# Decode scores: feature blocks and cache blocks on separate partition groups, 256 keys a product

## The chip, the cores and the metric

The kernel runs on one core of a Trainium2 chip, as one program. The metric is the device time of that core in microseconds, as the median over several runs. Beside it stands one execution that was taken with the hardware profiler; all durations of single instructions come from that one. The engines are TensorE (PE in the profile, with its weight loads as PEld), VectorE (DVE), ScalarE (ACT), GpSimd (POOL) and SyncE (SP).

## The reference

One layer of a hybrid decoder computes a prompt of 512 tokens and 8 sample requests of 4 tokens each: a first SwiGLU, a mixer that has a gated linear recurrence and a latent attention side by side, and a second SwiGLU. What the change touches is the latent attention of the sample tokens over their cache:

```python
s = (jnp.einsum('bqhr,bsr->bhqs', ql, c_kv) + jnp.einsum('bqhd,bsd->bhqs', qr, k_rope)).astype(jnp.float32) * scale
s = jnp.where(k_pos[None, None, None, :] <= qp[None, None, :, None], s, -jnp.inf)
p = jax.nn.softmax(s, axis=-1).astype(c_kv.dtype)
return jnp.einsum('bhqs,bsr->bqhr', p, c_kv)
```

For each of the 8 requests there are 16 queries (4 tokens times 4 heads) against 4096 cached keys. A key has 256 latent features and 64 rotary ones, and the latent part is also the value. The cache lies in pages, so its rows are gathered.

## The kernel before, in words

The decode attention is cut into 16 halves: half `n` has 2048 keys of request `n // 2`, as two gathered cache blocks of 1024 keys. In a block each of the 128 partitions holds 8 cache rows. The class `Half` has its steps, and a generator (`decode`) calls them in a fixed round: while half n is being scored, half n+1 is being transposed and half n-1 gets its softmax and its values.

- `turn` (L1480, tile `kh`): VectorE transposes the gathered rows in squares of 32, so that features come to lie on partitions. The 320 features are ten feature blocks of 32, taken two at a time in five stages; the rotary pair is stage 0. There are two transposes a stage (one per cache block), ten a half, and four `kh` buffers.
- `score` (L1492, tile `s`): TensorE multiplies 64 partitions of queries (two groups of 32 features, arranged as a block diagonal) by the transposed keys. One product has a weight of 64 x 32 and 128 moving columns (four cache rows of 32 keys). The array is used as eight separate tiles, two by partitions of the operands (`r`) and four by output partitions (`c`). All ten feature blocks accumulate into the same output partitions, and the four output groups are the four quarters of a half's keys. That makes 10 x 4 x 2 = 80 products a half, in two runs: stages 0 to 2 (48 products) and stages 3 and 4 (32). The profile records each of these products as two passes with a weight load each, so a run of 48 stands there as 96.
- The end of `score` (L1498, L1500): ScalarE copies the result of one `r` and VectorE that of the other out of PSUM into one tile `e` of 128 x 256 (the profile names it `q`, after the buffer in which it lies); VectorE takes the maximum (`mxh`).
- `peak` (L1504 to L1516): a product spreads the maxima (`pm`), VectorE reduces them and forms the bias (L1506, L1509), ScalarE takes the exponential (L1510), VectorE transposes it (`pt`, L1512), and 16 small copies place it into `pbuf`, twelve on ScalarE and four on VectorE.
- `value` (L1525, tile `o`): 16 products with `pbuf` as the weight and 256 latent columns of the gathered rows.

In between, the same engines work off the second SwiGLU of the prompt, whose generator is advanced beside the decode: products `acc` at L247, weight splits by ScalarE and VectorE (L220, L221), and the gating (`sit`, `sil`, L740 to L754). Later the prompt's remaining feed-forward columns follow as a block scheme with seven products (tiles X, Y, Z), in both kernels alike.

Each engine executes its own list in order. The order in these lists is set when the program is recorded: a layer below the code places an instruction by modelled durations, so an edit also moves its neighbours. `tc.issue_after` ties a transpose to the maximum before it. Nothing outside the decode differs in order between the two kernels, apart from line numbers.

Of the kernel before, what the change touches and what calls it, by code (L numbers as in the profile page):

```python
# [8 lines left out]
F32 = mybir.dt.float32  # L9
# [5 lines left out]
ALU = mybir.AluOpType  # L15
AX = mybir.AxisListType

P = 128
# [42 lines left out]
JS = ((8, 9), (0, 1), (2, 3), (4, 5), (6, 7))  # L61
# [45 lines left out]
def hybrid_step_kernel(  # L107
# [5 lines left out]
    nc = tc.nc  # L113
# [12 lines left out]
    def mk(shape, dt, tag, bufs=1, pool=None):  # L126
        return (pool or cur[-1]).tile(shape, dt, name=tag, tag=tag, bufs=bufs)
# [10 lines left out]
    def ps(name, tag="ps", own=False):  # L138
        if tag == "ps" and not own:
            tag = CYC[turns[0] % 4]  # L140
            turns[0] += 1
        return pp.tile([P, 512], F32, name=name, tag=tag, bufs=NPS[tag])
# [402 lines left out]
    with scope("ffn0") as pool:  # L545
# [4 lines left out]
        l, r = [u[:, lo4] for u in ux], [u[:, hi4] for u in ux]  # L550
# [56 lines left out]
        if True:  # L607
            if True:
                sst.close()
                st = stg.enter_context(tc.tile_pool(name="st", bufs=1, side="right", reuse_waits="tile"))  # L610
# [195 lines left out]
    with scope("mix") as mx_:  # L806
# [291 lines left out]
        with scope("at2"):  # L1098
# [166 lines left out]
            def qsplit(b):  # L1265
                q = qbd[b % 2]
                bs = slice(b * 16, b * 16 + 16)
                for g in range(4):
                    gs = slice(g * 32, g * 32 + 32)
                    (nc.scalar.copy if g % 2 else nc.vector.tensor_copy)(q[gs, :, g % 2 * 16 : g % 2 * 16 + 16], qrep[gs, :, bs])  # L1270
# [131 lines left out]
    with scope("dec"):  # L1402
# [48 lines left out]
        class Half:  # L1451
# [31 lines left out]
            def score(self, st):  # L1483
                q = qbd[self.b % 2]
                if st == 0:
                    self.s = [ps("s", own=True) for _ in range(2)]
                for jj, j in enumerate(JS[st]):
                    for c in range(4):
                        for r in range(2):
                            rs = slice(r * 64, r * 64 + 64)  # L1490
                            kh = self.kh[st][rs, c // 2, c % 2 * 4 : c % 2 * 4 + 4, jj]
                            nc.tensor.matmul(self.s[r][c * 32 : c * 32 + 32, :P], q[rs, j], kh, start=st + jj == 0, stop=st == len(JS) - 1 and jj == 1, skip_group_check=True)  # L1492
                if st == 1 and self.i and self.b + 1 < NB:
                    qsplit(self.b + 1)
                if st < len(JS) - 1:
                    return
                for r in range(2):
                    (nc.vector.tensor_copy if r else nc.scalar.copy)(self.e[:, r * P : r * P + P], self.s[r][:, :P])  # L1498
                self.mx = mk([P, 1], F32, "mxh", 2)
                self.top = nc.vector.tensor_reduce(self.mx, self.e, axis=AX.X, op=ALU.max)  # L1500

            def peak(self):
                pm = ps("pm", "pm")[:, :P]
                nc.tensor.matmul(pm, self.mx.broadcast_to([P, P]), ident, start=True, stop=True, skip_group_check=True)  # L1504
                m = m3[:, self.i, self.bs]
                nc.vector.tensor_reduce(m, pm.rearrange("p (g q) -> p q g", q=16), axis=AX.X, op=ALU.max)  # L1506
                mq = mk([P, 16], F32, "mq", 2)
                mb = mk([P, 1], F32, "mbd", 2)
                nc.vector.scalar_tensor_tensor(mq, m, -SCALE, selL, op0=ALU.mult, op1=ALU.mult, accum_out=mb)  # L1509
                nc.scalar.activation(self.e, self.e, AF.Exp, scale=SCALE, bias=mb, accum_out=Lc[:, self.i, 0, self.b : self.b + 1])  # L1510
                pt = mk([P, ROWS, 32], F32, "pt", 2)
                nc.vector.transpose(pt.rearrange("p a k -> p (a k)"), self.e)  # L1512
                for c in range(4):
                    for g in range(4):
                        src = pt[c * 32 : c * 32 + 32, g // 2 * 4 : g // 2 * 4 + 4, g % 2 * 16 : g % 2 * 16 + 16]
                        (nc.scalar.copy if g else nc.vector.tensor_copy)(self.p[g * 32 : g * 32 + 32, c // 2, c % 2 * 4 : c % 2 * 4 + 4, self.i * 16 : self.i * 16 + 16], src)  # L1516

            def value(self, mate, c):
                i = self.i
# [199 lines left out]
    with scope("ffn1") as pool:  # L1719
# [93 lines left out]
        st = stg.enter_context(tc.tile_pool(name="st2", bufs=1, side="right", reuse_waits="tile"))  # L1813
# [113 lines left out]
```

## Time and profile before

| What | Value |
|---|---|
| Median of 3 runs | 1243.49 us (1242.12 to 1243.71) |
| The profiled execution's own time | 1234.27 us |
| Its span in the trace | 1231.3 us |
| TensorE busy by the records | 98% of the span |
| VectorE, ScalarE, GpSimd busy | 80%, 57%, 8% |
| First and last score product | 724.9 us and 920.5 us of the span |

A row of grouped instructions reads: line, engine, operation, output and inputs, sizes, count, then the busy time in us and the mean of one in ns, and after the second bar the idle time of the engine before these instructions and what ended it. In the chain of waits and in the timeline the first two numbers are the start and the duration in us. In rows of windows each engine has its busy time and its count of instructions; the last three numbers are the granted clock of TensorE, the busy share of the DMA engines and GB/s.

### The profile page before, as it was taken

Reading aid. Unit: us, or ns where it says so; the run is one execution under the profiler, and the core shown is the slowest. Engines: PE = TensorE matmul, PEld = TensorE weight load, DVE = VectorE, ACT = ScalarE, POOL = GpSimd, SP = SyncE. Lnnn points to the kernel's source line nnn. Section 1 sums busy time; section 2 is a strip of 40 time slices with the busy share of each in tenths; the row PEclk is TensorE's granted clock in tenths of the full one; section 3 lists DMA queues with packets and bytes.
Section 4 is the critical chain, followed back from the end, with each engine's and each line's share of the span. In section 5 each row is a group of like instructions: output and inputs, shape, how many; then the busy total and the mean of one; then the engine's idle time right before and its main releaser. Section 6 shows DMA issues by size and latency. Waiting matters only on the chain.

```text
span 1231.3 us, 29416 instructions
## 1 busy us (share of the span) xinstructions
PE 1201.7 (98%) x12204; PEld 1109.0 (90%) x12204; DVE 987.3 (80%) x2008; ACT 705.6 (57%) x1527; POOL 94.2 (8%) x106
## 2 busy tenths in 40 slices
PE   8999999999999999999999999999999999999997
PEld 7999999999999989998998886767777999999996
DVE  7997787878678788886877789888985879768765
ACT  6765545454466754555758765656554455554373
POOL 0000000000000000000000123333320101000000
PEclk9999999999999999999999899999999999999999
DMA  6233333223254313333242686679765666833451
GB/s 240 69 121 103 104 104 97 93 88 101 78 200 136 105 59 103 88 97 114 83 139 88 212 304 224 231 264 357 266 243 184 248 256 236 212 105 115 107 148 73
DMA packets 80518, 190.69 MB, mean 155 GB/s; under 512 B 14064, under 2 KB 37648, under 8 KB 75904
## 3 DMA queue, kind: packets, MB, share of 16 engines
q1 hardware_dynamic: 58128, 115.50, 28.6%
q0 software_dynamic: 16368, 65.67, 16.4%
q10 hardware_dynamic: 5888, 7.65, 1.8%
q8 instruction: 95, 1.56, 0.5%
q14 instruction: 39, 0.32, 0.1%
HBM read 172.63 MB, written 16.16 MB: 153 GB/s over the span
## 4 chain that ended last, share of the span: by engine, by line
PE 79%; issue 7%; DVE 6%; DMA 4%; ACT 3%; POOL 0%; SPq 0%; DVEq 0%; ACTq 0%; POOLq 0%
PE acc L247 18%; PE dn L229 11%; PE Y L448 10%; PE acc L229 8%; PE X L448 7%; PE Z L448 7%; PE acc L1829 3%; PE acc L625 3%; PE s L1492 3%; PE o L1525 2%; DVE kh L1480 2%; DMA ma<-w_g 1%; PE pa L970 1%; DMA mb<-w_d 1%; DMA wraw<-w_g 1%
## 5 line engine op out<-in xcount | busy, mean ns | idle before, releaser
L247 PE MATMUL acc<-uh,wh 128*128 128x272 f32 (+2 forms) x496 | 160.7, 324 | 0.5 <-ACT uh L194 0.5
L247 PE MATMUL acc<-ul,wh 128*128 128x272 f32 (+2 forms) x496 | 156.4, 315 | 0.9 <-DVE ul L195 0.9
L247 PE MATMUL acc<-uh,wl 128*128 128x272 f32 (+2 forms) x496 | 155.5, 314 | 0.8 <-DVE wl L221 0.8
L229 PE MATMUL dn<-hh,dh 128*128 128x272 f32 x384 | 111.3, 290 | 0.1
L229 PE MATMUL dn<-hh,dl 128*128 128x272 f32 x384 | 110.7, 288 | 0.0
L229 PE MATMUL dn<-hl,dh 128*128 128x272 f32 x384 | 110.5, 288 | 0.0
L221 DVE TENSOR_TENSOR wl<-wraw,wh 128x1024 fp32r<-128x1024 f32 (+2 forms) x78 | 83.8, 1076 | 31.8 <-ACT wh L220 31.4
L220 ACT CAST wh<-wraw 128x1024 fp32r<-128x1024 f32 (+2 forms) x78 | 72.6, 932 | 59.8 <-PE acc L247 52.2
L247 PEld LDWEIGHTS acc<-uh,wh 128*128 128x128 f32 x496 | 93.4, 188 | 14.5 <-issue 10.2
L247 PEld LDWEIGHTS acc<-ul,wh 128*128 128x128 f32 x496 | 93.4, 188 | 7.0 <-issue 1.6
L247 PEld LDWEIGHTS acc<-uh,wl 128*128 128x128 f32 x496 | 93.3, 188 | 6.3 <-DVE wl L221 1.0
L229 PEld LDWEIGHTS dn<-hh,dh 128*128 128x128 f32 x384 | 72.3, 188 | 1.1 <-DVE ha L497 0.3
L229 PEld LDWEIGHTS dn<-hl,dh 128*128 128x128 f32 x384 | 72.4, 188 | 0.0
L229 PEld LDWEIGHTS dn<-hh,dl 128*128 128x128 f32 x384 | 72.2, 188 | 0.0
L157 ACT CAST wh<-wraw 128x512 fp32r<-128x512 f32 (+1 forms) x68 | 41.2, 644 | 44.2 <-PE Z L448 29.1
L157 ACT CAST sh<-wraw 128x512 fp32r<-128x512 f32 (+1 forms) x67 | 41.0, 650 | 31.2 <-PE Z L448 19.1
L157 ACT CAST dh<-wraw 128x512 fp32r<-128x512 f32 x48 | 29.7, 620 | 47.0 <-PE dn L229 43.7
L158 DVE TENSOR_TENSOR wl<-wraw,wh 128x512 fp32r<-128x512 f32 (+1 forms) x68 | 46.7, 718 | 6.3 <-ACT wh L157 5.1
L1516 ACT COPY pbuf<-pt 32x64 f32<-32x64 f32 x192 | 46.5, 242 | 7.9 <-DVE pt L1512 5.0
L1492 PE MATMUL s<-kh,q 64*32 64x128 f32 x2560 | 48.3, 273 | 2.5 <-issue 2.5
L1492 PEld LDWEIGHTS s<-kh,q 64*32 64x32 f32 x2560 | 37.3, 105 | 14.8 <-issue 9.2
L158 DVE TENSOR_TENSOR sl<-wraw,sh 128x512 fp32r<-128x512 f32 (+1 forms) x67 | 47.0, 726 | 1.4 <-ACT sh L157 0.8
(721 smaller groups left out, 4114.7 us busy)
## 6 DMA issues: line engine op xcount, KB each, us to landing
wraw<-w_u SPq DMA_DIRECT2D x44, 512.0 KB, 3.9
wraw<-w_g SPq DMA_DIRECT2D x43, 512.0 KB, 3.9
wraw<-w_d SPq DMA_DIRECT2D x24, 512.0 KB, 4.2
wraw<-w_in SPq DMA_DIRECT2D x24, 512.0 KB, 3.4
wraw<-w_o SPq DMA_DIRECT2D x16, 512.0 KB, 3.5
wraw<-w_d SPq DMA_DIRECT2D x16, 384.0 KB, 3.5
wraw<-w_d SPq DMA_DIRECT2D x16, 256.0 KB, 4.3
mA<-sit ACTq DMA_DIRECT2D x14, 256.0 KB, 4.7
```

Source lines behind the costliest of these rows:

```text
L157: nc.scalar.copy(hi, src)
L158: (eng or nc.vector).tensor_tensor(lo, src, f32(hi), op=ALU.subtract)
L220: nc.scalar.copy(wh[:, :kt], w[:, :kt])
L221: low[0] = nc.vector.tensor_tensor(wl[:, :kt], w[:, :kt], f32(wh[:, :kt]), op=ALU.subtract)
L229: nc.tensor.matmul(out, a, b, start=n == 0, stop=n == last)
L247: nc.tensor.matmul(acc[:, :n], a[:, k], b[:, k], start=k + i == 0, stop=k == kt - 1 and i == 2)
L448: nc.tensor.matmul(bank, a[p][:, k], b[q][:, k], start=first and k + n == 0, stop=k == 3 and n == 2, skip_group_check=True)
L625: nc.tensor.matmul(accs[x, d], wts[d][p][:, k], hs[k // 2][q][:, k % 2, x], start=k + n == 0, stop=k == nf - 1 and n == 2)
L1480: nc.vector.transpose(kh[:, g].rearrange("p a j k -> p a (j k)"), src)
L1492: nc.tensor.matmul(self.s[r][c * 32 : c * 32 + 32, :P], q[rs, j], kh, start=st + jj == 0, stop=st == len(JS) - 1 and jj == 1, skip_group_c ...
L1516: (nc.scalar.copy if g else nc.vector.tensor_copy)(self.p[g * 32 : g * 32 + 32, c // 2, c % 2 * 4 : c % 2 * 4 + 4, self.i * 16 : self.i * ...
L1829: nc.tensor.matmul(accs[x, d], wts[d][p][:, k], hs[k // 2][q][:, k % 2, x], start=k + n == 0, stop=k == nf - 1 and n == 2)
```

## The change

The score products are cut in another way. Even and odd feature blocks of a stage (`jj`) go to different output partitions, 0 to 63 and 64 to 127, and within these the two cache blocks (`g`) have 32 partitions each. A product then takes all eight rows of a cache block, 256 columns, and a half has 10 x 2 x 2 = 40 products instead of 80, still on eight tiles of the array. The two partial sums are added at the end: ScalarE copies the odd one out of PSUM into a new tile `odd` (64 x 256, once per `r`), and VectorE adds it to the even one while it writes `e`. The layout of `e` changes with it, and the placing takes 8 copies of twice the size (six on ScalarE, two on VectorE) instead of 16.

```diff
                 for jj, j in enumerate(JS[st]):
-                    for c in range(4):
+                    for g in range(2):
+                        c = (2 * jj + g) * 32
                         for r in range(2):
                             rs = slice(r * 64, r * 64 + 64)
-                            kh = self.kh[st][rs, c // 2, c % 2 * 4 : c % 2 * 4 + 4, jj]
-                            nc.tensor.matmul(self.s[r][c * 32 : c * 32 + 32, :P], q[rs, j], kh, start=st + jj == 0, stop=st == len(JS) - 1 and jj == 1, skip_group_check=True)
+                            nc.tensor.matmul(self.s[r][c : c + 32, : 2 * P], q[rs, j], self.kh[st][rs, g, :, jj], start=st == 0, stop=st == len(JS) - 1, skip_group_check=True)
...
+                odd = mk([64, 2, 2 * P], F32, "odd")
                 for r in range(2):
-                    (nc.vector.tensor_copy if r else nc.scalar.copy)(self.e[:, r * P : r * P + P], self.s[r][:, :P])
+                    nc.scalar.copy(odd[:, r], self.s[r][64:, : 2 * P])
+                    nc.vector.tensor_tensor(self.e[r * 64 : r * 64 + 64], self.s[r][:64, : 2 * P], odd[:, r], op=ALU.add)
...
-                for c in range(4):
-                    for g in range(4):
-                        src = pt[c * 32 : c * 32 + 32, g // 2 * 4 : g // 2 * 4 + 4, g % 2 * 16 : g % 2 * 16 + 16]
-                        (nc.scalar.copy if g else nc.vector.tensor_copy)(self.p[g * 32 : g * 32 + 32, c // 2, c % 2 * 4 : c % 2 * 4 + 4, self.i * 16 : self.i * 16 + 16], src)
+                for r in range(2):
+                    for g in range(2):
+                        for h_ in range(2):
+                            src = pt[(2 * r + g) * 32 : (2 * r + g) * 32 + 32, :, h_ * 16 : h_ * 16 + 16]
+                            to = self.p[(2 * r + h_) * 32 : (2 * r + h_) * 32 + 32, g, :, self.i * 16 : self.i * 16 + 16]
+                            (nc.scalar.copy if g + h_ else nc.vector.tensor_copy)(to, src)
```

On TensorE, at the second run of the first half (about 732 us of the span), the 32 score products stand in pieces between products of the feed-forward network. Before:

```order
L1492 MATMUL s<-kh,q_8213 32x128 x5
L247 MATMUL acc<-ul,wh 128x256
L247 MATMUL acc<-uh,wl 128x256
L247 MATMUL acc<-uh,wh 128x256
L1492 MATMUL s<-kh,q_8213 32x128 x2
```

Now:

```order
L1492 MATMUL s<-kh,q_8213 32x256
L247 MATMUL acc<-uh,wh 128x256
L1492 MATMUL s<-kh,q_8213 32x256 x4
L247 MATMUL acc<-ul,wh 128x256
L247 MATMUL acc<-uh,wl 128x256
L247 MATMUL acc<-uh,wh 128x256
L1492 MATMUL s<-kh,q_8213 32x256 x2
```

The run was five pieces (5, 2, 1, 1 and 23 products); it is now six (1, 4, 2, 1, 1 and 7). In the third half the second run also is in two pieces now, 2 and 14, where it was one of 32; in the second half a run that was in two pieces (42 and 6) is one of 24.

On VectorE, at the seventh half (about 807 to 810 us), from the transposed exponential to the next maximum, before:

```order
L1512 STREAM_TRANSPOSE pt<-q_8213 128x256
L1516 COPY pbuf<-pt 32x4x16 x4
L1480 STREAM_TRANSPOSE kh<-hb 128x512
L1480 STREAM_TRANSPOSE kh<-mb 128x512
L1480 STREAM_TRANSPOSE kh<-rraw 128x512 x2
L1498 COPY q_8213<-s 128x128
L1500 TENSOR_REDUCE mxh<-q_8213 128x1
```

Now:

```order
L1514 STREAM_TRANSPOSE pt<-q_8213 128x256
L1480 STREAM_TRANSPOSE kh<-hb 128x512
L1520 COPY pbuf<-pt 32x8x16 x2
L1480 STREAM_TRANSPOSE kh<-mb 128x512
L1480 STREAM_TRANSPOSE kh<-rraw 128x512 x2
L1500 TENSOR_TENSOR q_8213<-s,odd 64x256 x2
L1502 TENSOR_REDUCE mxh<-q_8213 128x1
```

Two copies stand between the transposes instead of four copies ahead of them, and two additions stand where one copy stood.

On ScalarE, at the same place, before:

```order
L1510 ACTIVATE q_8213<-q_8213,mbd 128x256
L1516 COPY pbuf<-pt 32x4x16 x12
L1498 COPY q_8213<-s 128x128
L1528 COPY q_8248<-o 128x256
L220 CAST wh<-wraw 128x512
```

Now:

```order
L1512 ACTIVATE q_8213<-q_8213,mbd 128x256
L1520 COPY pbuf<-pt 32x8x16 x6
L1499 COPY odd<-s 64x256 x2
L1532 COPY q_8248<-o 128x256
L220 CAST wh<-wraw 128x512
```

Six copies instead of twelve precede two copies of the new tile instead of one copy of the old one.

## The prediction

> **What bounds the kernel now.** I read the head of the page first, then the windows of the decode, then the chain of waits through them, then the groups of instructions and the DMA queues.
>
> ```profile
> span 1231.3 us, 29416 instructions
> PE 1201.7 (98%) x12204; PEld 1109.0 (90%) x12204; DVE 987.3 (80%) x2008; ACT 705.6 (57%) x1527; POOL 94.2 (8%) x106
> ...
> q8 instruction: 95, 1.56, 0.5%
> ```
>
> TensorE is busy 98% of the span, so an edit pays only as far as it shortens TensorE's list or the gaps in it. The windows show where the decode leaves gaps:
>
> ```profile
> 725.00:770.00 45.00, 41.27 (x696) 30.42 (x693) 42.97 (x103) 25.24 (x70) 12.11 (x11) 1.00 0.67 227
> 770.00:897.00 127.00, 123.82 (x2382) 91.30 (x2376) 110.86 (x252) 71.48 (x214) 40.63 (x41) 1.00 0.80 280
> 897.00:935.00 38.00, 37.34 (x591) 25.95 (x576) 29.20 (x72) 20.73 (x60) 6.32 (x8) 1.00 0.60 207
> 1070.00:1197.00 127.00, 127.00 (x1011) 126.43 (x1010) 96.53 (x175) 69.22 (x131) 5.12 (x4) 1.00 0.46 126
> ```
>
> The clock is full throughout. From 725 to 770 VectorE is busy 42.97 of 45 us and TensorE lacks 3.73 us: VectorE bounds there. From 770 to 897 TensorE lacks 3.18 us of 127 and VectorE is busy 87%. From 897 to 935 TensorE lacks 0.66 us. The last row, a stretch behind the decode, has no gap.
>
> In the chain of waits, the middle stretch is one TensorE piece after another:
>
> ```profile
> 782.12 1.52 PE s L1492 x96
> 783.64 2.98 PE acc L247 x12
> 786.62 1.08 PE s L1492 x64
> 787.70 1.86 PE o L1525 x32
> ...
> 821.90 2.01 issue
> ...
> 837.40 0.42 issue
> ...
> 872.68 0.50 issue
> ...
> 885.45 0.24 issue
> ```
>
> A half is a score run of 96 passes (1.52 us), products of the feed-forward network, a run of 64 (1.08), the values (1.86), more products. The four rows "issue" add up to 3.17 us, which is the whole gap of that stretch. No engine or tensor is waited for. What else began just ahead of them? In the view of the DMA queues, over 770 to 897 and then over four windows of 0.1 us each, from 821.5, 835.5, 870.7 and 883.2:
>
> ```profile
> q8 instruction: 19, 0.31, 1.0%
> ...
> q8 instruction: 1, 0.02, 59.8%
> q8 instruction: 1, 0.02, 55.4%
> q8 instruction: 1, 0.02, 65.0%
> q8 instruction: 1, 0.02, 59.4%
> ```
>
> Queue q8 carries TensorE's program. The page has 95 of its packets for 24408 TensorE records, one for 257; the stretch has 19 for 4758, one for 250. Each gap ends 2.3 to 2.4 us after the one packet in its window started (823.91 after 821.5, 837.82 after 835.5, 873.18 after 870.7, 885.69 after 883.2). So these are **waits for code**: the next block had not arrived. Dense score passes are what makes it late. Here a block lasts 127 / 19 = 6.7 us on average; in the stretch from 1070, at 1011 passes with their loads in 127 us, one lasts some 16 us, and nothing is lost.
>
> **The change, part by part.**
>
> *Score products, streaming.* Half as many, each with twice the columns. What does one cost?
>
> ```profile
> 805.10 1.59 PE L1492 MATMUL s<-kh,q 64*32 64x128 f32 x96
> ...
> 810.80 1.07 PE L1525 MATMUL o<-q,pbuf 128*32 128x256 f32 x16
> 811.68 1.05 PE L1525 MATMUL o<-ha,pbuf 128*32 128x256 f32 x16
> ```
>
> The 96 passes are 12 rounds of eight array tiles; less a tail of about 0.2 us, 1.32 / 12 = 0.11 us a round of 128 columns. The value products have 256 columns on four array tiles: 16 of them are four rounds, and the second group starts 0.88 us after the first, 0.22 us a round. So a round costs by its columns. Twelve rounds of 0.11 become six of 0.22, and I expect no gain in streaming. What changes is the ends: the last passes of a run of 96 come at the rate at which they are fed (1.32 / 96 = 14 ns each), which matters less with half as many, but the last round drains 0.11 us longer. For the run of 64, 1.08 us, I get 4 x 0.22 + 0.15 = 1.03; for the run of 96, 6 x 0.22 + 0.15 = 1.47. I take 0.06 us a run, 30 runs: **-1.8 us**, with bounds of -3.6 (0.12 each, if the feeding falls away wholly) and +3.0 (0.1 each, if only the longer drain is felt).
>
> By the Trainium skill (TensorEngine Tiling (Array Packing), Instruction Overhead) every matmul has an overhead of about 60 cycles; at 2.4 GHz that would make 1280 fewer passes worth 32 us, an estimate from that page, against 1.8 by the rows. This trace does not bear it out for passes on eight array tiles: 96 take 1.52 us, 16 ns each with everything in it.
>
> *Code.* 1280 passes and 1280 loads go, 2560 of TensorE's records, ten blocks. In the middle stretch a half now has about 450 records (19 x 250 over 10.5 halves) and will have about 290. Its densest 256 then take some 9 us, where the whole average was 6.7. In the four misses the packet started 0.2 to 2 us too late for a block that lasted about 6 us; with 9 us none of them is a miss. The four gaps are 3.17 us as recorded; a score pass is recorded with 273 ns though another could start 14 ns later, so each hides up to 0.25 us more: **-3.9 us**. Bounds: 0 (the misses only move to other blocks) and -3.9.
>
> The Trainium skill (Runtime: NRT & Kernel Launch, Instruction fetch mechanics) also has code arrive in blocks of 256 instructions, and says that the fetch is hidden by the rate of issue. By the rows above the blocks agree and the hiding does not; if it held, the four gaps would be something else and this term nothing (a rival below).
>
> *End of a score, placing.* The rows, from the groups between 724 and 921 us:
>
> ```profile
> L1516 ACT COPY pbuf<-pt 32x64 f32<-32x64 f32 x180 | 43.6, 242 | 7.7 <-DVE pt L1512 5.0
> L1516 DVE COPY pbuf<-pt 32x64 f32<-32x64 f32 x60 | 11.1, 184 | 1.0
> L1500 DVE TENSOR_REDUCE mxh<-q 128x1 f32<-128x256 f32 x15 | 6.3, 419 | 3.3 <-ACT q L1498 2.6
> L1498 DVE COPY q<-s 128x128 f32<-128x128 f32 x15 | 4.1, 275 | 3.4 <-PE s L1492 3.3
> L1498 ACT COPY q<-s 128x128 f32<-128x128 f32 x15 | 3.9, 262 | 10.0 <-PE s L1492 9.1 <-ACT sit L762 0.8
> L1270 ACT COPY q<-q 32x160 f32<-32x160 f32 x12 | 3.9, 322 | 0.3
> L1270 DVE COPY q<-q 32x160 f32<-32x160 f32 x12 | 2.9, 241 | 3.1 <-PE s L1492 3.0
> L1528 ACT COPY q<-o 128x256 f32<-128x256 f32 x7 | 2.6, 373 | 7.7 <-PE o L1525 7.7
> L788 DVE TENSOR_TENSOR sil<-sil,acc 128x256 f32<-128x256 f32 x1 | 0.4, 416 | 0.0
> ```
>
> ScalarE per half: two copies of 256 columns from PSUM (373 each) and six placing copies (at most 322, the 160-column form) for one of 262 and twelve of 242: 746 + 1932 - 262 - 2904 = -0.49 us. VectorE: two additions (416) and two copies (241) for one of 275 and four of 184: 832 + 482 - 275 - 736 = +0.30 us. And VectorE's list stands still longer at the first addition: from the last product to the maximum it was a copy and the reduction, 0.28 + 0.42; it becomes two ScalarE copies in sequence, the second addition and the reduction, 0.37 + 0.37 + 0.42 + 0.42, **0.9 us later**. Queued behind on VectorE are the next half's six transposes, for which TensorE's next score waits, and weight splits for L247.
>
> Who feels it? In the middle stretch:
>
> ```profile
> PEld s L1492 <- DVE kh L1480: 1.8, 5, 0.4
> ...
> 809.15 1.26 DVE L1480 STREAM_TRANSPOSE kh<-rraw 128x512 f32<-128x512 f32 x2
> 809.60 1.00 PEld L1492 LDWEIGHTS s<-kh,q 64*32 64x32 f32 x64 [0.37 <-DVE kh L1480]
> ```
>
> Some second runs start right as their last transposes end, so there VectorE has no slack. Against the 0.9 + 0.3 us stand the shorter placing ahead of these transposes (0.74 to 0.48) and the list in which the maximum of `pm` now goes ahead of gating work. Spread over 10.5 halves VectorE rises from 87% to about 90% of a stretch that also is 4 us shorter. I take **+1.0 us**, bounds 0 and +6 (seven halves at the full 0.9).
>
> *First halves.* TensorE's pieces:
>
> ```profile
> 731.71 0.36 PE s L1492 x10
> ...
> 732.62 0.34 PE s L1492 x4
> ...
> 733.51 0.33 PE s L1492 x2
> ```
>
> A piece of one product costs 0.33 us, nearly all of it the way in and out; with 256 columns it costs two rounds of 0.22 + 0.11, 0.55 us. The first half's second run has five such short pieces and one of seven, +1.2 us; the third half's extra piece +0.6, and the second half's joined run -0.3. That delays VectorE, which bounds there and has 0.3 us more to do in each of three halves; part is filled by a weight split that now stands ahead of the additions. I take **+1.5 us** (0 to +3).
>
> *Last half.* Its values wait for placing copies, in the waits from 925 to 935:
>
> ```profile
> PEld o L1525 <- ACT pbuf L1516: 2.5, 4, 0.7
> ```
>
> TensorE's own gap there is the 0.66 us of the third window; six copies instead of twelve take it: **-0.6 us** (0 to -0.7).
>
> Later rows move along whole: the order outside the decode is unchanged.
>
> *Sum:* -1.8 - 3.9 + 1.0 + 1.5 - 0.6 = **-3.8 us**. The profiled execution took 1234.27 us, 2.97 more than its span; it would take 1230.5. The median of the runs shown is 9.2 us above that execution; I carry the difference over unchanged, 1243.49 - 3.8 = **1239.7 us**, and count the 9 us as a reason for a wider range.
>
> **The rivals.**
>
> *VectorE takes the pace* (slower). The 0.9 us later maximum costs in every half where transposes end as the score starts. For: 87% busy, 42.97 of 45 us in the first stretch, and the row at 809.60. Against: `PEld s` waits for `kh` are 1.8 us in the whole decode, and the additions come right after a run, with 5 us until the next. It decides once the slack of the next score is under 0.9 us in more than about five halves. Price at ten halves: 0.9 x 10 = +9, the code gap then is half hidden (-2), -1.8, +1.5 - 0.6: 1243.49 + 6 = about 1249; at six halves about 1246.
>
> *The code gaps stay* (nothing visible). Lateness comes from the DMA queues (80% busy there), and a block boundary may again fall into a run. For: one packet started only 0.1 us before TensorE stood still. Against: the arithmetic of 9 us a block. Time: 1243.49 + 0.1, about 1243.6.
>
> *Cost by product, not by column.* Then half of the 48.3 us of score passes goes, 1219 us:
>
> ```profile
> L1492 PE MATMUL s<-kh,q 64*32 64x128 f32 x2560 | 48.3, 273 | 2.5 <-issue 2.5
> ```
>
> Against it stands the value run, whose 256-column rounds take twice the time. The overhead in the Trainium skill (TensorEngine Tiling (Array Packing), Instruction Overhead) points to this case too.
>
> *More than forecast.* ScalarE's lighter placing and VectorE's shorter copies also close the gaps of the first stretch (3.73 us): without the +2.5 us of the two losses and with 1 us of these gaps, -7.3, about 1236.
>
> **How the numbers follow.** Forecast 0.49, VectorE 0.14, code gaps stay 0.20, by product 0.02, more than forecast 0.15. A change under 0.2%, 2.5 us, can't be told from none here. Faster by more than that (below 1241.0): 0.41 of the forecast's 0.49, all of the "more" and "by product": 0.58. Slower by more (above 1246.0): 0.10 of VectorE's share and 0.02 of the code gaps': 0.12. The rest, 0.30, is within. Range: 1235.5 to 1245.0; above lies most of VectorE's case (0.1), below about 0.08. The forecast's own range is 1237.0 to 1242.5.
>
> **What would show it.** The four "issue" gaps between 770 and 897 gone, 12 or 13 packets of q8 there per 127 us instead of 19; score runs of 48 and 32 passes at about 1.47 and 1.03 us; TensorE's gap from 725 to 770 grown by 1 to 2 us; VectorE's idle time before the additions about 0.5 us a half, put down to `odd`. Wrong would be: score runs clearly shorter than 1.4 us, gaps of 2 us with a code packet ahead of them, or `PEld s` waits for `kh` of more than 5 us.

## The result, and the profile after

The changed kernel takes 1235.63 us in the median of 8 runs (1232.3 to 1241.7) and the kernel before 1243.97 us beside it (8 runs, 1242.12 to 1246.48): a ratio of 0.9934, 95% interval 0.9913 to 0.9954, or 8.3 us less. Forecast were 3.8 us less. The two profiled executions are equal, though: 1234.27 us before, 1233.6 us now, spans 1231.3 and 1231.5. So there are two questions: what became of the decode, and why does the trace show no gain? First the head of the page of the changed kernel, then its windows over the decode (columns as before):

```profile
span 1231.5 us, 26728 instructions
PE 1201.8 (98%) x10924; PEld 1093.9 (89%) x10924; DVE 990.5 (80%) x1992; ACT 695.5 (56%) x1447; POOL 94.9 (8%) x106
...
q8 instruction: 85, 1.39, 0.5%
```

```profile
725.00:770.00 45.00, 41.36 (x419) 26.87 (x401) 42.54 (x96) 23.54 (x58) 11.31 (x11) 1.00 0.64 220
770.00:897.00 127.00, 126.73 (x1558) 83.00 (x1550) 113.53 (x246) 64.28 (x161) 42.77 (x42) 1.00 0.79 279
897.00:935.00 38.00, 37.69 (x376) 25.83 (x373) 32.70 (x76) 19.07 (x45) 5.71 (x8) 1.00 0.61 210
```

TensorE's gap in the middle stretch fell from 3.18 to 0.27 us. The page has ten code packets fewer, and the DMA queues of the stretch have 13 instead of 19:

```profile
q8 instruction: 13, 0.21, 0.7%
```

Pieces of the chain of waits there:

```profile
774.42 1.02 PE s L1492 x32
775.45 1.86 PE o L1529 x32
...
781.90 1.46 PE s L1492 x48
```

No long "issue" row is left, and the runs are 1.46 and 1.02 us long, 1.52 and 1.08 before. The groups of instructions between 724 and 925 us, by form:

```profile
L1520 ACT COPY pbuf<-pt 32x128 f32<-32x128 f32 x90 | 26.7, 297 | 8.1 <-DVE pt L1514 6.9
L1500 DVE TENSOR_TENSOR q<-s,odd 64x256 f32<-64x256 f32 x32 | 13.3, 417 | 10.1 <-ACT odd L1499 5.4 <-issue 4.1
L1499 ACT COPY odd<-s 64x256 f32<-64x256 f32 x32 | 10.5, 370 | 13.8 <-PE s L1492 7.5 <-PE o L1529 5.1 <-issue 0.4
L1520 DVE COPY pbuf<-pt 32x128 f32<-32x128 f32 x30 | 6.1, 204 | 0.2
```

The durations are those that the prediction took from neighbours: 417 ns an addition (416 forecast), 370 a copy (373), 297 and 204 a placing copy (322 and 241).

So the decode became shorter, and the time was given back later. TensorE's waits for DMAs at L1322, a matrix-vector product of the sample tokens (tile `sr`), between 940 and 1040 us show where. The kernel before:

```profile
PE sr L1322 <- DMA mb<-w_d: 1.3, 1, 1.3
PE sr L1322 <- DMA ma<-w_u: 1.0, 2, 0.5
```

and the changed kernel:

```profile
PE sr L1322 <- DMA ma<-w_u: 2.9, 2, 1.7
...
PE sr L1322 <- DMA mb<-w_d: 1.0, 1, 1.0
PE sr L1322 <- DMA ma<-w_g: 0.9, 1, 0.9
```

In this stage GpSimd loads two buffers of weights (L1314, `ma` and `mb`, 2.1 MB together) as soon as the products before have read them; TensorE works on feed-forward columns meanwhile, and the next `sr` starts when the load has landed. One such round in the timeline, first before, then now:

```profile
981.52 0.70 POOL L1314 DMA_DIRECT2D ma<-w_u  x1 [9.19 <-PE sr L1322]
...
987.29 0.41 PE L1322 MATMUL sr<-ma,sq 128*32 128x128 f32 x4 [0.55 <-DMA ma<-w_u]
```

```profile
979.49 0.70 POOL L1314 DMA_DIRECT2D ma<-w_u  x1 [10.15 <-PE sr L1322]
...
986.36 0.41 PE L1322 MATMUL sr<-ma,sq 128*32 128x128 f32 x4 [1.65 <-DMA ma<-w_u]
```

The same load takes 5.77 us from issue to product before and 6.87 us now, although its lines are the same in both kernels. What else runs then? The DMA queues in a window of 0.1 us around the start of that round's code packet: in the kernel before from 982.65 us on (the packet starts 1.2 us after the load's issue),

```profile
q8 instruction: 1, 0.02, 58.0%
```

and in the changed kernel from 981.9 us on (2.5 us after the issue):

```profile
q0 software_dynamic: 13, 0.05, 135.5%
q8 instruction: 1, 0.02, 68.9%
```

Before, the block of code starts ahead of the data, whose first packet starts 1.4 us after the issue in both; now it starts while the data flow. By the packets, 90% of the load has landed 6.9 us after its issue before and 6.8 us now, but the last packet at 7.8 us before and at 8.8 us now. That is the theory to be tested: **the change moved the blocks of TensorE's code, and a block that falls into a load makes the load's last packets late.**

### The profile page after: what moved, and what is told of

The parts are those of the page before. It is cut to its first block, busy times and chain, and to the rows that moved or that the text cites. A ratio compares the mean times of both kernels' runs of the same rounds, so it can differ in the third digit from the quotient of the medians.

```text
span 1231.5 us, 26728 instructions
## 1 busy us (share of the span) xinstructions
PE 1201.8 (98%) x10924; PEld 1093.9 (89%) x10924; DVE 990.5 (80%) x1992; ACT 695.5 (56%) x1447; POOL 94.9 (8%) x106
## 4 chain that ended last, share of the span: by engine, by line
PE 80%; issue 7%; DVE 6%; DMA 4%; ACT 3%; POOL 0%; DVEq 0%; SPq 0%; ACTq 0%; POOLq 0%
PE acc L247 19%; PE dn L229 11%; PE Y L448 10%; PE acc L229 8%; PE X L448 6%; PE Z L448 6%; PE acc L1833 3%; PE acc L625 3%; PE s L1492 3%; PE o L1529 2%; DMA ma<-w_g 1%; DVE kh L1480 1%; PE pa L970 1%; DMA mb<-w_d 1%; PE s L1220 1%
## 5 line engine op out<-in xcount | busy, mean ns | idle before, releaser
L1492 PE MATMUL s<-kh,q 64*32 64x256 f32 x1280 | 47.3, 382 | 0.2 <-DVE kh L1480 0.2
L1472 POOL DMA_INDIRECT rraw<-pool_r,idx x32 | 34.4, 1075 | 143.8 <-DVE kh L1480 106.9
L500 ACT COPY tq<-X 128x272 f32<-128x272 f32 x31 | 12.0, 387 | 53.6 <-PE X L448 53.0
```

The costliest lines, as they stand in the source:

```text
L1472: nc.gpsimd.indirect_dma_start(rraw.rearrange("p a r -> p (a r)"), None, pool_r, off)
L1492: nc.tensor.matmul(self.s[r][c : c + 32, : 2 * P], q[rs, j], self.kh[st][rs, g, :, jj], start=st == 0, stop=st == len(JS) - 1, skip_group_ ...
```

## The experiments

Times are medians; each ratio is to the kernel before, run beside it on the same chip. "Decode" is the time from the first score product to the first `sr` product behind it, "rounds" that from the first `sr` product to the tenth group of them, both read off each profiled execution. (The decode isn't read to the last half's values, since the changed kernel has products ahead of these values that the kernel before has behind them.)

| Run | Time, us | Kernel before, us | Ratio (95% interval) | Decode, us | Rounds, us |
|---|---|---|---|---|---|
| first profile before | | | | 221.13 | 73.10 |
| first profile of the change | | | | 219.08 | 76.25 |
| b1 | 1233.44 | 1233.27 | 0.9993 (0.998 to 1.0007) | 222.66 | 73.34 |
| a1 | 1230.03 | 1233.27 | 0.9972 (0.9958 to 0.9986) | 215.19 | 77.56 |
| e_128 | 1237.11 | 1233.27 | 1.0028 (1.0015 to 1.0041) | 222.63 | 75.99 |
| e_16 | 1232.2 | 1233.27 | 0.9996 (0.9987 to 1.0006) | 217.99 | 74.20 |
| a_48 | 1225.14 | 1233.54 | 0.9936 (0.9922 to 0.995) | 215.32 | 72.66 |
| a_128 | 1225.37 | 1233.54 | 0.9938 (0.9925 to 0.9952) | 215.40 | 72.50 |
| b_208 | 1234.34 | 1233.54 | 1.0011 (1.0001 to 1.0022) | 222.88 | 73.89 |
| a_48r | 1225.91 | 1234.14 | 0.9939 (0.9923 to 0.9956) | 215.42 | 72.18 |
| a1r | 1230.94 | 1234.14 | 0.998 (0.9968 to 0.9992) | 216.16 | 76.25 |
| c_ind | 1225.29 | 1234.14 | 0.9933 (0.9917 to 0.9949) | 216.14 | 72.18 |
| b_128 | 1232.38 | 1234.14 | 0.9985 (0.9973 to 0.9996) | 221.83 | 72.64 |
| b_248 | 1248.22 | 1245.09 | 1.003 (1.0016 to 1.0043) | 232.74 | 76.10 |

The four groups of rows from b1 on that share a "kernel before" are four jobs, each on a chip of its own.

### Both kernels again: b1, a1, a1r

No edit. Expected of b1:

> The kernel before, unchanged, profiled and timed once more, because its one profiled execution (1234.3 us) lies 9.7 us below its median (1244.0) while the changed kernel's profiled execution (1233.6) lies within its own runs. Theory A (the code waits differ from run to run): its spans vary with the number and length of TensorE gaps marked as issue in the decode; a new profile of about 1244 us would show some 13 us of such gaps instead of 3.2 us. Rival B (the 10 us lie outside the decode, in the weight stages or in the clock): the decode from 770 to 897 us takes the same 127 us and the rest is longer.

of a1:

> The changed kernel, unchanged, profiled and timed once more. Theory: the decode is about 3 us shorter than in the kernel before's first profile, with no code wait between 770 and 897 us, and the time is 1232 to 1238 us. Rival: the time is that of the kernel before within 2 us, and the 8 us between the medians were a matter of the chip.

and, two jobs later, of a1r:

> The changed kernel unchanged, once more. Theory: 3 us below the kernel before, as in the job before last (8 us below on the first chip); sr comes 6.4 to 7.2 us after the load's issue in the first three rounds, and where a round keeps TensorE waiting for about 2 us or more, the granted clock is then 0.5 for some 4 us. Rival: no give-back in the rounds and 8 us below the kernel before, as in the first measurement.

On these two chips the change is worth 3.2 us each time (1233.27 to 1230.03, 1234.14 to 1230.94), not 8.3. The decode of the two repeats is 5.0 to 7.5 us shorter than in the two profiles of the kernel before, and the rounds are 2.9 to 4.5 us longer, so the give-back belongs to the kernel. Neither theory of b1 held: its profile takes 1233.61 us and its median is 1233.44, so there is no difference of 10 us to explain on this chip. a1 is below its forecast of 1232 to 1238 us; its decode is shorter and without code waits as expected. b1 has five code waits instead of four in the chain of waits from 770 to 897, of which three are:

```profile
821.45 1.55 issue
836.50 0.74 issue
...
886.29 0.48 issue
```

All five make 4.5 us instead of 3.2, mostly at the same products: these waits vary from run to run in number and size. In a1 and a1r none is left.

### The products cut in two again: e_128

```diff
-                for jj, j in enumerate(JS[st]):
-                    for g in range(2):
+                for u in range(2):
+                  for jj, j in enumerate(JS[st]):
+                    for g in range(2):
...
-self.s[r][c : c + 32, : 2 * P], q[rs, j], self.kh[st][rs, g, :, jj]
+self.s[r][c : c + 32, u * P : u * P + P], q[rs, j], self.kh[st][rs, g, u * 4 : u * 4 + 4, jj]
```

Everything else is the changed kernel's. (The scores of this form are not complete, so its attention is not the reference's; passes, copies and sizes are as they should be.)

> The changed kernel with each product cut into two of 128 keys: same new layout, same additions and eight placing copies, but 80 products a half again. Theory (fewer passes are what pays, by code waits and by the ends of the runs): score runs are 1.52 and 1.08 us again, some 19 code packets stand between 770 and 897 us, waits for code of 2 to 4 us or more come back, and the time is 4 to 8 us above the changed kernel, 1239 to 1244 us. Rival (the layout, the additions and the larger copies pay): it stays within 1.5 us of the changed kernel.

It is 7.1 us above the changed kernel, and the code waits are back (chain of waits, 770 to 897):

```profile
821.85 2.37 issue
839.43 0.68 issue
874.86 0.76 issue
887.98 0.64 issue
```

These four are 4.45 us. The runs are 1.52 and 1.08 us again, 0.06 each on 30 runs, 1.8. The rest is something the forecast did not know, and the windows behind the first wait show it (the third number from the end is the granted clock):

```profile
821.85:824.22 2.37, 0.00 (x1) 0.00 (x0) 0.88 (x2) 0.00 (x0) 1.88 (x2) 1.00 0.66 192
824.30:826.00 1.70, 1.70 (x27) 0.70 (x30) 1.02 (x4) 1.08 (x4) 0.00 (x0) 0.52 0.90 302
826.00:828.00 2.00, 2.00 (x24) 0.79 (x16) 1.97 (x5) 0.20 (x1) 0.94 (x1) 0.55 0.18 68
```

After a wait of 2.37 us TensorE gets half its clock for 3.4 us (from 828 us on it is 1.00 again), which costs about 1.7 us more by an estimate, half of that stretch. So this undoes the change's gain in the decode (222.63 us, 222.66 in b1), by number of passes alone: the code waits and the ends of the runs are two parts of it, as forecast, and the slow clock behind a long wait is a third. The rounds, though, stay long (75.99 us), with as many blocks of code as the kernel before has.

### Sixteen placing copies again: e_16

```diff
-                            (nc.scalar.copy if g + h_ else nc.vector.tensor_copy)(to, src)
+                            for a in range(0, ROWS, 4):
+                                src = pt[(2 * r + g) * 32 : (2 * r + g) * 32 + 32, a : a + 4, h_ * 16 : h_ * 16 + 16]
...
+                                (nc.scalar.copy if g + h_ else nc.vector.tensor_copy)(to, src)
```

> The changed kernel with 16 placing copies of the old size (twelve on ScalarE, four on VectorE) instead of eight: only that part is undone. Theory: the placing is worth 0.6 us at the last half and at most 1 us elsewhere, so the time is 0 to 2 us above the changed kernel, with the gaps ahead of the last half's values back. Rival (lighter ScalarE and VectorE lists carry the gain): 4 to 8 us above it.

2.2 us above the changed kernel, just over the top of the range. In the profiles its decode is 2.8 us longer than a1's and its rounds are 3.4 us shorter, and the spans are equal (1229.5 and 1229.8 us). 1.8 of the 2.8 us lie ahead of the fourth half's values, where TensorE's order differs a little, too. The other half of the expectation failed: the gaps ahead of the last half's values are not back. The first value products of the last half, in the kernel before and then in e_16:

```profile
928.91 1.41 PE L1525 MATMUL o<-dx,pbuf 128*32 128x256 f32 x16 [0.26 <-ACT pbuf L1516]
```

```profile
927.64 0.67 PE L1602 MATMUL pb<-q,ones 128*128 128x256 f32 x2 [0.29 <-DVE q L1600]
928.24 1.07 PE L1530 MATMUL o<-dx,pbuf 128*32 128x256 f32 x16
```

With sixteen copies, too, they run in 1.07 us and wait for no copy. What closes the gap is the new place in TensorE's list: the products `pb` and a feed-forward product now stand ahead of these values, and stood behind them.

### Where the blocks of code are cut: a_48, a_128

TensorE stands idle for the first 5.8 us. Tiny products there (32 x 1 elements, four records each with their loads) move every later block of 256 records and nothing else: behind the first 12 us all engines have the same order as without them. Twelve of them are 48 records:

```diff
             pr = ps("pr", PRT)
+            for k in range(0 if x else 12):
+                nc.tensor.matmul(pr[k % 4 * TS : k % 4 * TS + TS, :1], ones[:, :TS], ones[:, :1], start=True, stop=True, skip_group_check=True)
             for k in range(KD):
```

> The changed kernel with 12 tiny products (32 x 1, 48 records of TensorE with their loads) put ahead of the first statistics product, where TensorE stands idle until 5.8 us. Nothing else in any engine's order differs behind the first 12 us. They move every 256-instruction block of TensorE's code 48 records ahead. Theory (a code packet of 16 KB that lands in the middle of a 2.1 MB load of the sample's matrix-vector rounds holds one DMA engine up, and the round starts late): in the changed kernel the packet starts 2.4 to 2.8 us after the load is issued and the next sr product comes 6.4 to 7.2 us after the issue; by the record count the packets now start some 3 us earlier, at -1.0 to 0 us, ahead of the data, and sr comes 5.5 to 5.9 us after the issue, so the first three rounds are 2.5 to 3 us shorter together. The decode stays without code waits (densest block 8.8 us by the changed kernel's records against 8.2). Time 2 to 3 us below the changed kernel's own. Rival (the later rounds are slow for another reason, such as the rows' place in the buffers or other DMA traffic): rounds as before, 6.4 to 7.2 us, time unchanged within 0.7 us.

and 32 of them are 128 records:

> As the run with 48 records, but 32 tiny products, 128 records, half a block. Theory: the code packets of the sample's rounds start some 5 us earlier than in the changed kernel, 2.5 to 3 us ahead of the load's issue, so outside the load; sr 5.5 to 5.9 us after the issue and 2.5 to 3 us gained over the first three rounds; the decode has one block of 7.6 us, nearer to the limit, so a code wait of up to 0.5 us may come back at about 790 us. Time 2 to 3 us below the changed kernel's own. Rival: rounds and time as in the changed kernel.

Both hit the theory's side, and more than was asked: 8.4 and 8.2 us below the kernel before, where the changed kernel is 3.2 below. The same round in the timeline with 48 records, and the DMA queues around its code packet (from 975.35 us on; the packet starts 0.07 us after the issue):

```profile
975.32 0.70 POOL L1314 DMA_DIRECT2D ma<-w_u  x1 [9.19 <-PE sr L1322]
...
980.82 0.41 PE L1322 MATMUL sr<-ma,sq 128*32 128x128 f32 x4 [0.28 <-DMA ma<-w_u]
```

```profile
q8 instruction: 1, 0.02, 80.9%
```

The load's last packet lands 7.47 us after the issue, and `sr` starts after 5.50 us. All first three rounds take 5.3 to 5.9 us, in both runs. The rounds are 3.6 to 5.1 us shorter than the changed kernel's three profiles have them, and the decode keeps its 215 us without a code wait. The larger end of this goes with the windows of a1, where the wait in the second round was the longest:

```profile
982.60:984.57 1.97, 0.00 (x0) 0.03 (x1) 0.73 (x2) 0.00 (x0) 0.00 (x0) 1.00 0.96 393
984.60:986.00 1.40, 1.40 (x8) 1.11 (x9) 0.00 (x0) 0.00 (x0) 0.00 (x0) 0.56 0.07 26
986.00:988.00 2.00, 2.00 (x11) 2.00 (x10) 0.00 (x0) 0.00 (x0) 0.00 (x0) 0.50 0.02 6
```

The wait of 1.97 us is followed by half the clock here, too.

a_48r is a_48 on another chip, beside the changed kernel:

> The run with 48 records once more, beside the changed kernel and the one with independent copies. Theory: 4.5 to 5.5 us below the changed kernel in the same job, 1225 to 1226 us if the kernel before is at 1233 to 1234 there; rounds of the sample 5.5 to 5.9 us after the load's issue, no code waits in the decode. Rival (the gain of the first time was drift between jobs): within 1 us of the changed kernel.

1225.91 against 1230.94 us: 5.0 us less, as expected. This kernel beats both others.

### The same shift in the kernel before: b_208, b_128, b_248

The same edit in the kernel before, with 52, 32 and 62 tiny products (208, 128 and 248 records; the last is a whole block less 8 records).

> The kernel before with 52 tiny products ahead of the first statistics product (208 records, so blocks of code are cut 208 records ahead, or 48 records later seen from the block that was there). They may take longer than the idle 5.5 us and delay the start by 0 to 4 us; so the stages are to be read and not the time alone. Theory: in the sample's rounds the code packet, at +0.9 to +1.2 us after the load's issue in the kernel before, now starts at about +4 to +5 us, in the middle of the data; sr comes 6.5 to 7 us after the issue instead of 5.6 to 5.8, 2.5 to 3.5 us lost over the first three rounds: the give-back appears without the change. In the decode the code waits stay in kind but move: TensorE again stands still where its record count is 193 above a multiple of 256, and the score runs at which this is so are others than 821.9, 837.4, 872.7 and 885.4 us; by the records the densest blocks then are at 805, 855, 904 and 916 us. Rival: the rounds stay at 5.6 to 5.8 us, the code waits stay at the same products.

> The kernel before with 32 tiny products (128 records) ahead. Theory: the code waits in the decode move again (by the records the densest blocks are at 793, 844, 892 and 905 us) and add up to 3 to 4.5 us, as at the two other positions; the packets of the sample's rounds start outside the loads (1 to 1.5 us ahead of the issue or over 7 us behind it) and sr comes 5.4 to 5.9 us after the issue. Time within 2 us of the kernel before, 6 to 9 us above the changed kernel with 48 records. Rival (the changed kernel's gain at 48 records comes from the shift, which the kernel before lacked): the kernel before gains 4 us or more by it, too.

> The kernel before with 62 tiny products (248 records) ahead: one whole block of TensorE's code less 8 records, so that the blocks are cut almost where they were. Theory of the sample's rounds: by the records the block boundary is passed there 3.4 to 3.7 us after the load's issue, as in the changed kernel (3.1 in the kernel before), so that the code packet starts at +1.5 to +2.7 us, inside the data; sr then comes 6.2 to 7.2 us after the issue in two or three of the first three rounds instead of 5.6 to 5.8, and from the first sr product to the tenth group it takes 74.5 to 77 us instead of 73.1: the give-back without the change. Rival (the give-back belongs to the changed kernel's order or buffers): 72.6 to 73.6 us. In the decode the code waits come back within a few products of those of the kernel before (about 822, 837, 873 and 885 us). Time 0 to 4 us above the kernel before.

*Code waits in the decode.* Counted in TensorE's records (products, weight loads, and the instructions in its list that wait for a semaphore), each code wait of the kernel before falls where the count is 193 or 194 above a multiple of 256. With 208 records more they stand at other products; the chain of waits from 770 to 930 in b_208:

```profile
811.06 1.11 issue
...
825.07 0.60 issue
...
860.52 0.45 issue
...
874.64 0.86 issue
```

All of these are at 193 again, and each ends 2.2 to 2.4 us after a code packet's start; the ones at the products of the kernel before (821.9, 837.4, 872.7 and 885.4 us) are gone. With 128 records they stand at 797.57, 846.38, 859.51 and 895.13 us (0.57, 0.66, 0.47 and 1.32 us), at 193 too. So they are waits for code, and the kernel before has 3 to 4.5 us of them at each of the positions tried on these chips, the changed kernel none at 0, 48 and 128 records. The rival, that the kernel before lacked only the shift, falls: b_128 gains 1.8 us by it, a_128 some 5.

*The rounds.* In b_208 I had the packet in the middle of the load, at +4 to +5 us. It started at +7.2 to +7.7 us, when 99% of the data had landed, and the rounds stayed at 5.4 to 5.8 us. The forecast of the packet's place was wrong; the link between place and round holds. (Its time gains nothing, since a later load of this stage, `mb<-w_d`, was late by 2.65 us; the same one is late by 1.3 us in the first profile before and by 2.5 us in b_128. That one I cannot put down to code.) b_128 has the packet 0.9 to 1.5 us ahead of the issue and rounds of 5.4 to 5.8 us. b_248 is the crossed test: the kernel before, with its code cut so that the packet falls into the load. Its second round, and the DMA queues around the packet at 997.6 us, 3.8 us after the issue:

```profile
993.90 0.70 POOL L1314 DMA_DIRECT2D ma<-w_u  x1 [10.08 <-PE sr L1322]
...
1000.82 0.41 PE L1322 MATMUL sr<-ma,sq 128*32 128x128 f32 x4 [1.69 <-DMA ma<-w_u]
```

```profile
q0 software_dynamic: 12, 0.05, 119.2%
q8 instruction: 1, 0.02, 59.2%
```

The first three rounds take 6.73, 6.92 and 5.92 us, and the stage 76.10 us instead of 73.10: the give-back without the change, 3.1 us in the time (1248.22 against 1245.09 us beside it) and 3.0 us in the stage against the first profile before (the kernel before was not traced on this chip). Of the four code waits that were expected near their old products one came (1.77 us at 827.26 us, at a count of 193); the other pauses in this decode are of another kind (below).

TensorE's count at the issue of the first of these loads, again above a multiple of 256, orders the rounds of all profiles:

| Count | Profiles | Code packet after the issue, three rounds, us | Rounds, us |
|---|---|---|---|
| 135 | b_248 | 1.4 to 3.9 | 76.10 |
| 137 | the three of the changed kernel, e_128 | 1.2 to 2.8 | 75.99 to 77.56 |
| 140 | e_16 | 1.3 to 1.7 | 74.20 |
| 144 | first profile before, b1 | 0.9 to 1.3 | 73.10 and 73.34 |
| 184 | a_48, a_48r, c_ind | -0.3 to 0.5 | 72.18 to 72.66 |
| 8 and 15 | a_128, b_128 | -1.5 to -0.6 | 72.50 and 72.64 |
| 95 | b_208 | 7.2 to 7.7 | 73.89 |

### The addition without its operand: c_ind

```diff
-                    nc.vector.tensor_tensor(self.e[r * 64 : r * 64 + 64], self.s[r][:64, : 2 * P], odd[:, r], op=ALU.add)
+                    nc.vector.tensor_copy(self.e[r * 64 : r * 64 + 64], self.s[r][:64, : 2 * P])
```

> The changed kernel with 48 records ahead (the 12 tiny products), and in each score's end VectorE copies the even partial sum out of PSUM instead of adding the odd one to it; ScalarE still makes its two copies, but nobody waits for them. The odd feature blocks are so left out of the scores. The order of all engines is unchanged. Measures the term of VectorE's later maximum (forecast +1.0 us, bounds 0 to +6). Theory: the wait for ScalarE's copies (4.5 us of VectorE's idle time over 15 halves in the trace with 48 records) is hidden, since TensorE has other products to do until the next score: 0 to 1 us below the run with 48 records. Rival (VectorE sets the pace at the score's end): 3 us or more below it.

0.6 us below a_48r, and its decode is no shorter (216.14 against 215.42 us). But the experiment did not do what it was meant to. The groups of its trace, between 724 and 925 us:

```profile
L1500 DVE COPY q<-s 64x256 f32<-64x256 f32 x32 | 13.3, 417 | 7.2 <-ACT odd L1499 6.5
```

VectorE's copies still wait for ScalarE's, though they no longer read `odd`; that the recording layer orders the two readers of the tile `s` would explain it. So it shows only that a copy takes as long as the addition, 417 ns, and leaves the price of the wait unmeasured.

## Why the prediction was right, and where it was not

The range of 1235.5 to 1245.0 holds the 1235.63 us, by 0.13 us, and "faster" was the likeliest side. But the 8.3 us of the first measurement are more than twice the 3.8 forecast, and where 3.2 us came out, on two chips, the sum was met partly by luck: the decode gained more than forecast, and a loss that the sum did not have took half of it back.

*Score runs, -1.8.* Right: 1.46 and 1.02 us were measured where 1.47 and 1.03 were forecast, and e_128 gives the 0.06 us a run back. A round costs by its columns.

*Code, -3.9.* Right in mechanism and size. The waits vanish with half the records, come back when the products are cut in two, and move with the blocks. The kernel before has 3.0 to 4.5 us of them; the 0.25 us that each was to hide beside that was not measured.

*First halves, +1.5.* The sign is right, the size was less. From the first score product to the values of the fourth half it is 62.8 us before and 63.3 now; with six shorter runs (-0.4) the loss is 0.9. But TensorE's gap did not grow by 1 to 2 us as forecast: 3.64 us from 725 to 770, 3.73 before. The loss lies in TensorE's busy time.

*VectorE's later maximum, +1.0.* Seen in part. VectorE does stand idle for `odd`, 5.4 us in the group above, 0.34 us a half, while TensorE's waits of `s` for `kh` stay small: 2.5 us in the same stretch. The maximum itself keeps TensorE waiting in the ninth half, at 838 us, in five profiles (a1, a1r, a_48, a_48r, a_128): 0.4 to 1.4 us, 0.7 in the mean, and in none of the kernel before. The largest, from the waits of a1r between 724 and 945 us:

```profile
PE pm L1506 <- DVE mxh L1502: 1.4, 1, 1.4
```

In a1r ScalarE's copies `odd` are late there, behind a copy `sit` that waits 3.9 us for a DMA.

*Last half, -0.6.* The gap is gone, but not for the reason given: e_16 shows that the place of the values in TensorE's list did it, and not six copies instead of twelve. The term was too small as well. From the fifteenth half's values to the first `sr` product it is 25.3 us before and 24.1 now, -1.2, of which two shorter runs are 0.1.

*The decode as a whole.* It takes 222.1 us before (mean of the first profile, b1, b_128, b_208) and 215.5 now (mean of the five named above), -6.6 where the terms said -3.8. That is near the rival "more than forecast" (-7.3). The runs, the recorded code waits (3.5 in the mean), the first halves, the maximum and the last half make -1.8 - 3.5 + 0.9 + 0.7 - 1.1 = -4.8. The other 1.8 us are put down to no row; by the prediction's estimate of 0.25 us a wait, what the code waits hid is 1 us of it.

*"Later rows move along whole: the order outside the decode is unchanged."* **This step failed.** The order is unchanged, the time is not: the rounds of the sample take 76.7 us in the mean of the changed kernel's three profiles and 73.2 in the two of the kernel before, +3.5, because blocks of code fell into loads. It is not the ten blocks fewer that moved them. 2560 records are ten whole blocks, which by themselves leave every later cut where it was: products and weight loads stand at 51 above a multiple of 256 at the first load's issue in both kernels. What differs is the instructions that wait, 86 ahead of that issue where the kernel before has 93. So the cuts come 7 records later in the work, and b_248, 9 below the kernel before in the table of counts, pays the same without the change. -6.6 and +3.5 make -3.1, which is the -3.2 of the two chips. With the blocks out of the loads in both kernels the change is worth about 6.5 us (a_48r 1225.91, b_128 1232.38 beside it).

*Why the first measurement says 8.3.* Not settled. The last job shows a chip on which the kernel before takes 1245.09 us, as in the first measurement, and there the decode alone is longer: 232.74 us in b_248 against 222. Its chain of waits has stretches such as no trace of the other three chips shows:

```profile
813.94 0.33 issue
814.27 0.44 PE s L1492 x5
814.71 0.33 issue
```

Dense passes stand still after every few records, at no fixed count, and the score group rises from 48.3 to 54.3 us:

```profile
L1492 PE MATMUL s<-kh,q 64*32 64x128 f32 x2560 | 54.3, 274 | 6.8 <-issue 6.6
```

The first profile of the changed kernel has pauses of this kind as well; its decode is 219.08 us where the other six profiles with 256 keys a product and eight copies have 215.2 to 216.2. If such pauses go with the number of dense passes, a kernel with half as many gains more on such a chip. That is argued; both kernels were not traced on one such chip, and what makes the pauses is open.

## What to carry to other kernels

An edit moves everything behind it against whatever runs on a fixed count, and the engine's own code is such a thing: here 7 waiting instructions fewer in one engine's list decided over 3.5 us in a stage that nobody touched. Compare the stages behind the change too, not only the one that was edited, and between points that have the same work ahead of them in both kernels. When a load's last packets are late though its bytes are not, look for what else went through the DMA queues in its middle. A dozen idle products ahead of the kernel can shift the blocks of code, and cost nothing where the engine waits anyway.

## What the runs showed of the hardware

- A code block of 16 KB is one packet, of 0.9 to 1.7 us in the first three rounds of the sample. Started 1.24 to 3.9 us after the issue of a 2.1 MB load, it let the last packets land at 8.0 to 9.4 us there (7.8 once, at 1.28 us) instead of 7.2 to 7.8, while 90% landed at 6.7 to 7.0 us either way. That fits one of the 16 DMA engines being held up; the trace does not name the engine.
- TensorE goes on 2.2 to 2.5 us after a code packet's start, at a record count of 193 or 194 above a multiple of 256, in every code wait looked at. The instructions that wait for a semaphore count too.
- A TensorE gap of about 2 us can cost almost as much again: after gaps of 1.98, 2.37 and 2.65 us the granted clock was 0.5 for 3.41 us. After 2.01, 2.17 and 2.51 us, and after every gap of 1.2 to 1.8 us, it stayed at 1.00. Nor is such a gap needed: ahead of the decode, at 697 to 700 us, the clock fell to 0.5 for 3.41 or 6.83 us in 13 of the 14 profiles of either kernel, where TensorE works in short pieces and no gap is over 0.93 us. The Trainium skill (TensorE: Matmul & The Clock Gate, Part 1: The HAM clock gate) has a half-rate state and a window of about 3.4 us that runs freely, so that its position against the work matters; the length of the slow stretch and the mixed outcome near 2 us agree with that, while an idle time of a whole window was not needed here.
- The kernel before took 1233 to 1234 us on three chips and 1245 on a fourth. The one trace from the fourth (b_248) is 15.5 us longer in its span than the first profile before: 11.6 of it in the decode, 3.0 in the rounds.
